# A routed-expert layer: one expert's overflow slots in straight code, the loop for all other overflow behind the last weight load

## The chip, the cores and the metric

The kernel runs on one core of a Trainium2 chip. The metric is the device time of one execution in microseconds (us), the median of several runs. The engines are PE (TensorE: matmuls; its weight loads are listed as PEld), DVE (VectorE), ACT (ScalarE), POOL (GpSimd) and SP (SyncE, which here only issues DMA transfers). Each engine works through its own queue of instructions in order, and engines wait for each other by semaphores.

## The reference

One decoder layer of 256 tokens and width 1024: a first sub-layer of token mixers, a cross-attention, and then the routed experts, which this change is about. Each token picks 4 of 32 experts:

```python
logits = (xf @ w_router) + b_router
top_val, top_idx = lax.top_k(logits, TOP_K)          # 4 of 32
gates = softmax(top_val)
# for each expert e, for the tokens that picked it:
h = x[tok] @ w1[e] + b1[e]                           # 1024 -> 2048
h_gate = min(h[:, :1024], 7); h_up = clip(h[:, 1024:], -7, 7)
act = h_gate * sigmoid(1.702 * h_gate) * (h_up + 1)
acc[tok] += (act @ w2[e] + b2[e]) * gate             # 1024 -> 1024
x = layer_norm(alpha * x + acc)
```

All is float32. The weights of one expert are 8 MB (w1) and 4 MB (w2).

## The kernel before

The experts are worked through in 16 pairs, in straight code. In its main pass each expert serves up to 64 tokens (`CAP`), its slots 1 to 64. A one-hot matrix `oh` (L1281) gathers the pair's tokens into `xg` (L1080), `expert_in` multiplies them with w1 (`pgt` and `pup`, L1103, with the bias first, L1097), `expert_swiglu` and `expert_turn` make the activation `at` on DVE, ACT and PE (L1119 to L1131), `expert_out` multiplies with w2 (`py`, L1144), and the pair's result goes into the accumulator `acc` by a matmul with the gates and an addition (`pc`, L1162 and L1163). In the last pair the accumulator is taken into the matmuls' own sums instead (`final`, `pc_last`, L1153 and L1158), and the last layer norm follows.

The weights come in pieces of 2 MB, six for an expert (four of w1, two of w2), into ten slots that are used in rotation (`RINGS`). SP issues all of these loads in order (L1023), each when the slot's former piece has been used. Behind the last piece stand two loads for the layer norm (`ln3`).

An expert may be picked by more than 64 tokens. Positions 2 to 31 are fixed, but which expert stands at position `PX` = 17 is decided at run time: the fullest one is swapped there (`swap`), so its overflow can be done while its weights are in the slots. Before, this was done in branches. At position 17, `overflow_in` (L1228) and `overflow_out` (L1271) run if its count exceeds 64: slots 65 to 96 by `extra_in` and `extra_out` (32 slots wide, tiles named with an `x` behind: `xsx`, `xtx`, `pgtx`, `pupx`, `pyx`, `pc0x`, `pc1x`), and, in an inner branch (L1229), five more blocks of 32 if it exceeds 96. After that pair `overflow_others` (L1240 to L1268) asks whether the highest count of the other experts exceeds 64 (L1241). Only then does a loop over the 32 experts run, which loads an expert's weights once more from POOL's queue and does its overflow in blocks. All five engines read the count (`tab_i`) and branch at L1241; an engine that doesn't enter jumps over its part of the loop's body, and adds to its semaphores what it left out.

Within straight code a scheduler decides each engine's order: it may issue a piece of work early where its inputs are ready. Across a branch it moves nothing.

Of the kernel before, what the change touches and what calls it, by code (L numbers as in the profile page):

```python
# [27 lines left out]
E = 32  # L28
# [19 lines left out]
def layer_kernel(ctx, tc, a, out, dbg=None):  # L48
# [955 lines left out]
    order = pool(ctx, "order")  # L1004

    Rp = order.tile([P, 2 * NT, E], F32, name="Rp")
    tab_i = order.tile([1, 2 * E + 2], I32, name="tab_i")
    cnt_i, idx_i = tab_i[:, 0:E + 2], tab_i[:, E + 2:]


    RINGS = [(ring2, "ring2")] * 3 + [(ring, "ring"), (ring3, "r0"), (ring3, "r1"), (ring, "ring"), (ring, "ring"),
# [28 lines left out]

    def w2_views(e):
        return [([P, 4, D], of(w2v, e)[c]) for c in range(2)]

    BRANCH = (mybir.EngineType.PE, mybir.EngineType.DVE, mybir.EngineType.Activation)

    class Main:

# [41 lines left out]
    def expert_in(v, sel, xg, chunks, nm, after=None):  # L1089


        n, W = v.n, v.W
        ps2 = v.gate("pgt" + nm), v.gate("pup" + nm)
        sel = sel.to_broadcast([3 * E, n])
        for i, ps in enumerate(ps2):
            for j in range(v.J):
                nc.tensor.matmul(ps[j * n:(j + 1) * n, :W], sel, b1[:, i * D + j * W:i * D + (j + 1) * W],  # L1097
                                 start=True, stop=False)
        for c, w in enumerate(chunks):
            for i, ps in enumerate(ps2):  # L1100
                for kk in range(2):
                    for j in range(v.J):
                        nc.tensor.matmul(ps[j * n:(j + 1) * n, :W], xg[:, 2 * c + kk, :],  # L1103
                                         w[:, kk, i * D + j * W:i * D + (j + 1) * W],
                                         start=False, stop=c == 3 and kk == 1)
            if after and c == 0:
                after()
        return ps2
# [17 lines left out]
    def expert_turn(v, hu, at, nm):  # L1126
        W = v.W
        pt = v.bank("pt" + nm)
        for u in range(W // P):
            nc.tensor.transpose(pt[:, u * P:(u + 1) * P], hu[:, u * P:(u + 1) * P], ident)  # L1130
        nc.scalar.activation(at, pt[:, :W], AF.Copy, scale=0.5)  # L1131
# [18 lines left out]
    def final(t, half, alloc):  # L1150

        finals[t, half] = ps = alloc(f"pc{t}{half}_last")
        nc.tensor.matmul(ps, ident, acc[:, t, half * 512:half * 512 + 512], start=True, stop=False)  # L1153

    def add_out(v, ct, y, rows, t, cols, nm):
        if finals:
# [48 lines left out]
    def extra_out(at, ct, w2, nm):  # L1205
        extra_add(expert_out(extra, at, w2, False, nm), ct, nm)
# [13 lines left out]
    def columns(e):  # L1220

        es = slice(e, e + 1)
        return Rp[:, 0:NT, es], Rp[:, NT:2 * NT, es], sel3p[:, es]

    def overflow_in(e, cnt, w1, w2):

        state = extra_tiles(f"x{e}")
        with tc.If(cnt > CAP):  # L1228
            with tc.If(cnt > CAP + 32):  # L1229
                for base in range(CAP + 32, T, 32):  # L1230
                    nm = f"x{e}_{base}"
                    extra_in(*columns(e), w1, base, *state, nm)
                    extra_out(*state, w2, nm)
            extra_in(*columns(e), w1, CAP, *state, f"x{e}")
        return state

    def overflow_others():

        pool = [mybir.EngineType.Pool]
        most = nc.values_load(cnt_i[0:1, E + 1:E + 2])  # L1240
        with tc.If(most > CAP):  # L1241
            with tc.For_i(0, E) as i:
                here = bass.ds(i, 1)
                cnt = nc.values_load(cnt_i[0:1, here])
                with tc.If(cnt > CAP):
                    idx = nc.values_load(idx_i[0:1, here], engines=pool, min_val=0, max_val=E - 1)
                    own = md.tile([P, 2 * NT, 1], F32, tag="own", bufs=1, name="own")
                    sel = md.tile([3 * E, 1], BF16, tag="ownsel", bufs=1, name="ownsel")
                    nc.vector.tensor_copy(own, Rp[:, 0:2 * NT, here])
                    nc.vector.tensor_copy(sel, sel3p[:, here])  # L1250

                    def again(nm, shape, view):
                        w = ring3.tile(shape, F32, tag="r3", name="again" + nm)
                        nc.gpsimd.dma_start(w, view)
                        return w

                    def block(base):
                        nm = f"z{base}"
                        state = extra_tiles(nm)
                        extra_in(own[:, 0:NT], own[:, NT:], sel, (again(nm, s, w) for s, w in w1_views(idx)), base,  # L1260
                                 *state, nm)
                        py = expert_out(extra, state[0], (again(nm, s, w) for s, w in w2_views(idx)), False, nm)
                        extra_add(py, state[1], nm)

                    block(CAP)
                    with tc.If(cnt > CAP + 32):
                        for base in range(CAP + 32, T, 32):
                            block(base)  # L1268

    def overflow_out(e, cnt, state, w2):  # L1270
        with tc.If(cnt > CAP):  # L1271
            extra_out(*state, w2, f"x{e}")

    def prepare(pr):

# [55 lines left out]

    swap(few[0:1], few[0:1])
    nc.vector.tensor_copy(idx_i, few[0:1, 0])
    nc.vector.tensor_copy(cnt_i[0:1, E:E + 1], few[0:1, 1, PX:PX + 1])
    nc.vector.memset(few[0:1, 1, PX:PX + 1], 0.0)
    nc.vector.tensor_copy(cnt_i[0:1, 0:E], few[0:1, 1])
    nc.vector.tensor_reduce(kmax[0:1], few[0:1, 1], axis=AX.X, op=OP.max)
    nc.vector.tensor_copy(cnt_i[0:1, E + 1:E + 2], kmax[0:1])

# [22 lines left out]
    for pr in range(E // 2):  # L1364
        xg, og, rest = nxt
        Y = [md.tile([P, 512], F32, tag=f"Y{i}", bufs=1, name=f"Y{i}_{pr}") for i in range(2)]
        for i in range(2):
            e = 2 * pr + i
            w1 = []
            ex = e if e < NS else nc.values_load(idx_i[0:1, e:e + 1], engines=[mybir.EngineType.SP], min_val=0,  # L1370
                                                 max_val=E - 1)
            for c, (sh, view) in enumerate(w1_views(ex)):
                w1.append(echunk(sh, view, f"w1_{e}_{c}"))
                if e == 1 and c == 0:
                    acc_start(*acc_load())
            w2 = [echunk(sh, view, f"w2_{e}_{c}", 4 if e == E - 1 and c else 1)
                  for c, (sh, view) in enumerate(w2_views(ex))]
            nm = f"{e}"
            cnt = nc.values_load(cnt_i[0:1, E:E + 1], engines=BRANCH) if e == PX else None
            if e == E - 1:  # L1380
                for t, half in ((0, 0), (0, 1), (1, 0)):
                    final(t, half, bank)
            ps2 = expert_in(main, (sel3 if e < NS else sel3p)[:, e:e + 1], xg[:, :, i * CAP:(i + 1) * CAP], w1, nm, rest if e == 0 else None)
            hu = expert_swiglu(main, ps2, nm)
            if e == E - 1:
                final(1, 1, gbank)
            at = main.tile("at" + nm)
            state = overflow_in(e, cnt, w1, w2) if e == PX else None

            with tc.issue_after(nc.cur_bb.bb.instructions[-1]) if e == PX else ExitStack():  # L1390
                expert_turn(main, hu, at, nm)
            if i == 0:
                cts = [md.tile([P, T], F32, tag=f"ct{j}", bufs=1, name=f"ct{j}_{pr}") for j in range(2)]
                for j in range(2):
                    gate_rows(main, og[:, :, j:j + 2].rearrange("p t a s -> p t (a s)"), cts[j], f"{pr}_{j}")
            py = expert_out(main, at, w2, i == 1, nm)
            for j in range(2):
                rows = slice(j * CAP, (j + 1) * CAP)
                nc.scalar.activation(Y[j ^ i][rows, :], py[rows, :], AF.Copy)  # L1399
            if i == 1:  # L1400
                if pr + 1 < E // 2:
                    nxt = prepare(pr + 1)
            if e == PX:
                overflow_out(e, cnt, state, w2)
        for t in range(NT):
            for half in range(2):
                add_out(main, cts[half], Y[half], slice(0, P), t, slice(half * 512, half * 512 + 512), f"{half}_{pr}")

        if pr == PX // 2:
            overflow_others()  # L1410

    ln3 = slot([P, 2, D], "ln3")
    nc.sync.dma_start(ln3[:, 0], a["ln3_g"].to_broadcast([P, D]))
    nc.sync.dma_start(ln3[:, 1], a["ln3_b"].to_broadcast([P, D]))
    st = md.tile([P, NT, 2, 6], F32, tag="ln_st", bufs=1, name="ln3st")
    for t in range(NT):
        for half in range(2):
# [76 lines left out]
```

## Time and profile before

| | |
|---|---|
| median of 3 runs | 1528.34 us (1526.82 to 1529.77) |
| profiled execution | 1527.18 us, span 1525.5 us, mean granted PE clock 0.977 |
| busy PE / PEld / DVE / ACT / POOL | 1396.3 / 778.6 / 577.1 / 427.3 / 8.8 us |
| moved by DMA | 480.21 MB, of it 475.72 MB in the queue that SP feeds |

All of the rows come from one profiled execution. Times in a timeline are us from the span's start; a timeline's row has start, length, engine, line, operation and tiles, and in brackets how long the engine stood idle before it and what released it. PE's matmuls overlap in a pipeline, so that starts tell more than lengths. L with a number is a line of the kernel.

### The profile page before, as it was taken

The numbers are of one execution on the slowest core, as the hardware profiler recorded it, in microseconds if no ns is written. First come the engines' busy times: TensorE is split into PE (matmuls) and PEld (weight loads), VectorE is DVE, ScalarE is ACT, GpSimd is POOL, SyncE is SP. The second block draws the span as 40 slices with busy tenths as digits, with TensorE's granted clock in tenths as the row PEclk, the third lists the DMA queues.
The fourth block names the chain that finished last, engine by engine and source line by source line (L and its number), as shares of the span: only waits on it lengthen the run. The fifth ranks groups of instructions, "written<-read, shape, count | busy, mean of one in ns | idle before, by whom it ended". The sixth has DMA issues, their size and how long they took to land. (4 is left out here: it accounts for less than half of the span.)

```text
span 1525.5 us, 21509 instructions
## 1 busy us (share of the span) xinstructions
PE 1396.3 (92%) x8749; PEld 778.6 (51%) x8750; DVE 577.1 (38%) x1434; ACT 427.3 (28%) x925; POOL 8.8 (1%) x25
## 2 busy tenths in 40 slices
PE   7999999999999999999999999978689889899895
PEld 6788978799988633333333333323223323323331
DVE  6587869667875532112112112111112112112113
ACT  6575757665574311101101101100001101101111
POOL 0000000000000000000000000000000000000000
PEclk9999999999999999999999999997899999999998
DMA  7243334266854899999999999990799999999995
GB/s 278 96 167 112 111 112 148 75 225 206 304 215 159 318 404 418 418 416 416 418 418 416 417 417 418 416 389 2 291 418 417 418 415 418 418 417 415 418 418 219
DMA packets 91290, 480.21 MB, mean 315 GB/s; under 512 B 4336, under 2 KB 6928, under 8 KB 56144
## 3 DMA queue, kind: packets, MB, share of 16 engines
q1 hardware_dynamic: 90368, 475.72, 78.0%
q0 software_dynamic: 816, 3.04, 0.7%
q8 instruction: 71, 1.16, 0.3%
q14 instruction: 35, 0.29, 0.1%
HBM read 477.69 MB, written 1.05 MB: 314 GB/s over the span
## 5 line engine op out<-in xcount | busy, mean ns | idle before, releaser
L1103 PE MATMUL pgt<-w,xg 128*64 128x512 f32 x1024 | 250.6, 602 | 36.3 <-DMA w<-in_w_exp_in_dram 36.3
L1144 PE MATMUL py<-w,at 128*64 128x512 f32 x1024 | 242.5, 623 | 14.7 <-ACT at L1131 14.7
L1103 PE MATMUL pup<-w,xg 128*64 128x512 f32 x1024 | 248.6, 598 | 0.0
L1119 DVE TENSOR_SCALAR hg<-pgt 128x512 f32<-128x512 f32 x32 | 22.1, 692 | 511.4 <-PE pgt L1103 511.4
L1103 PEld LDWEIGHTS pgt<-w,xg 128*64 128x64 f32 x1024 | 71.6, 137 | 191.6 <-issue 135.3
L1103 PEld LDWEIGHTS pup<-w,xg 128*64 128x64 f32 x1024 | 75.6, 139 | 149.2 <-issue 149.2
L1120 ACT ACTIVATE th<-hg 128x512 f32<-128x512 f32 x32 | 20.1, 629 | 469.7 <-DVE hg L1119 469.7
L1144 PEld LDWEIGHTS py<-w,at 128*64 128x64 f32 x1024 | 72.2, 142 | 154.2 <-issue 129.7
L1399 ACT ACTIVATE Y<-py 64x512 f32<-64x512 f32 x64 | 37.9, 592 | 180.4 <-PE py L1144 180.0
L1162 PE MATMUL pc<-Y,ct 128*128 128x512 f32 x120 | 55.4, 604 | 2.7 <-ACT Y L1399 2.7
L1131 ACT ACTIVATE at<-pt 128x512 f32<-128x512 f32 x32 | 19.1, 597 | 94.9 <-PE pt L1130 94.9
L1163 DVE TENSOR_TENSOR acc<-acc,pc 128x512 f32<-128x512 f32 x60 | 41.1, 685 | 8.2 <-PE pc L1162 6.5
L1097 PEld LDWEIGHTS <-sel3p 96*64 96x64 bf16 (+1 forms) x128 | 10.5, 109 | 52.3 <-issue 52.3
L1097 PE MATMUL pup<-b,sel3p 96*64 96x512 bf16 x60 | 12.2, 389 | 25.4 <-DVE hu L1122 25.4
L1162 PEld LDWEIGHTS pc<-Y,ct 128*128 128x128 f32 x120 | 21.6, 189 | 26.9 <-issue 14.8
L334 DVE SCALAR_TENSOR_TENSOR u<-ps_g,feat,u 128x255 f32<-128x255 f32 (+2 forms) x72 | 33.1, 474 | 0.3
L1130 PE MATMUL pt<-ident,hu 128*128 128x128 f32 x128 | 21.5, 290 | 10.2 <-DVE hu L1123 10.2
L1121 DVE SCALAR_TENSOR_TENSOR hg<-th,hg 128x512 f32<-128x512 f32 x32 | 22.1, 692 | 22.3 <-ACT th L1120 22.3
L230 PE MATMUL ps_g<-xT,wg_0h 128*128 128x256 f32 x96 | 28.1, 293 | 0.9 <-ACT wg_0h L219 0.9
L232 PE MATMUL ps_g<-xT,wg_0l 128*128 128x256 f32 x96 | 28.1, 293 | 0.3 <-DVE wg_0l L220 0.3
L231 PE MATMUL ps_g<-xT,wg_0h 128*128 128x256 f32 x96 | 28.0, 292 | 0.0
L230 PE MATMUL ps_g<-xT,wg_1h 128*128 128x256 f32 x96 | 27.8, 290 | 0.0
(944 smaller groups left out, 2535.5 us busy)
## 6 DMA issues: line engine op xcount, KB each, us to landing
w<-in_w_exp_in_dram SPq DMA_DIRECT2D x128, 2048.0 KB, 25.8
w<-in_w_exp_out_dram SPq DMA_DIRECT2D x63, 2048.0 KB, 31.0
w_g<-in_w_in_dram SPq DMA_DIRECT2D x7, 2048.0 KB, 7.7
w_d<-in_w_in_dram SPq DMA_DIRECT2D x4, 2048.0 KB, 7.8
w_gt<-in_w_in_dram SPq DMA_DIRECT2D x4, 2048.0 KB, 7.8
w_dv<-in_w_in_dram SPq DMA_DIRECT2D x2, 2048.0 KB, 12.2
w_diffo<-in_w_diff_o_dram SPq DMA_DIRECT2D x2, 2048.0 KB, 11.7
w_gdno<-in_w_gdn_o_dram SPq DMA_DIRECT2D x2, 2048.0 KB, 8.3
```

What stands on the lines that cost most here:

```text
L230: nc.tensor.matmul(ps, h[:, kk, :], src[0][:, k, :], start=k == 0, stop=False)
L231: nc.tensor.matmul(ps, h[:, kk, :], src[1][:, k, :], start=False, stop=False)
L232: nc.tensor.matmul(ps, l[:, kk, :], src[0][:, k, :], start=False, stop=k == KT - 1)
L334: m1 = nc.vector.scalar_tensor_tensor(y[:, sh:], ps[:, :T - sh], convw[:, blk, tau:tau + 1], y[:, sh:], op0=OP.mult, op1=OP.add)
L1097: nc.tensor.matmul(ps[j * n:(j + 1) * n, :W], sel, b1[:, i * D + j * W:i * D + (j + 1) * W], start=True, stop=False)
L1103: nc.tensor.matmul(ps[j * n:(j + 1) * n, :W], xg[:, 2 * c + kk, :], w[:, kk, i * D + j * W:i * D + (j + 1) * W], start=False, stop=c == 3 ...
L1119: nc.vector.tensor_scalar(hg, pgt, 7.0, None, op0=OP.min)
L1121: nc.vector.scalar_tensor_tensor(hg, th, 1.0, hg, op0=OP.add, op1=OP.mult)
L1144: nc.tensor.matmul(py[j * n:(j + 1) * n, :W], at[:, k % U, (k // U) * n:(k // U + 1) * n], w[:, kk, hf * W:(hf + 1) * W], start=k == 0, st ...
L1162: nc.tensor.matmul(pc, ct[rows, t * P:(t + 1) * P], y[rows], start=True, stop=True)
L1163: nc.vector.tensor_tensor(acc[:, t, cols], acc[:, t, cols], pc, op=OP.add)
L1399: nc.scalar.activation(Y[j ^ i][rows, :], py[rows, :], AF.Copy)
```

## The change

The extra block of position 17 (slots 65 to 96) stands in straight code and always runs; its count is no longer asked. What was in the inner branch, an own count over 96, is left to the loop for the others: the count of position 17 counts there if it exceeds 96 and is zero otherwise, and then the positions of its tokens up to 96 are set to zero so that they are not done twice. That loop, with its If, moves from behind pair 8 to the place in front of expert 31's matmuls, behind the issue of all weight loads and of the two norm loads. Its If is laid out with `preferred_fallthrough_block=False`: the path that doesn't enter the loop comes first, and leaves by a jump over the body. Expert 31's matmuls are queued behind the last of three `final` matmuls.

```diff
-    def overflow_in(e, cnt, w1, w2):
+    def overflow_in(e, w1):
         state = extra_tiles(f"x{e}")
-        with tc.If(cnt > CAP):
-            with tc.If(cnt > CAP + 32):
-                for base in range(CAP + 32, T, 32):
...
-            extra_in(*columns(e), w1, CAP, *state, f"x{e}")
+        extra_in(*columns(e), w1, CAP, *state, f"x{e}")
         return state
     def overflow_others():
-        most = nc.values_load(cnt_i[0:1, E + 1:E + 2])
-        with tc.If(most > CAP):
+        nc.vector.scalar_tensor_tensor(Rp[:, 0:NT, PX], Rp[:, 0:NT, PX], float(CAP + 32), Rp[:, 0:NT, PX],
+                                       op0=OP.is_gt, op1=OP.mult)
+        most = nc.values_load(cnt_i[0:1, E:E + 1])
+        with tc.If(most > CAP, preferred_fallthrough_block=False):
...
                     def again(nm, shape, view):
-                        w = ring3.tile(shape, F32, tag="r3", name="again" + nm)
+                        p, tag = RINGS[nslot[0] % len(RINGS)]
+                        w = p.tile(shape, F32, tag=tag, name="again" + nm)
-    def overflow_out(e, cnt, state, w2):
-        with tc.If(cnt > CAP):
-            extra_out(*state, w2, f"x{e}")
...
-    nc.vector.tensor_copy(cnt_i[0:1, E:E + 1], few[0:1, 1, PX:PX + 1])
-    nc.vector.memset(few[0:1, 1, PX:PX + 1], 0.0)
+    own = few[0:1, 1, PX:PX + 1]
+    nc.vector.scalar_tensor_tensor(own, own, float(CAP + 32), own, op0=OP.is_gt, op1=OP.mult)
...
-            cnt = nc.values_load(cnt_i[0:1, E:E + 1], engines=BRANCH) if e == PX else None
             if e == E - 1:
+                ln3 = slot([P, 2, D], "ln3")
+                nc.sync.dma_start(ln3[:, 0], a["ln3_g"].to_broadcast([P, D]))
+                nc.sync.dma_start(ln3[:, 1], a["ln3_b"].to_broadcast([P, D]))
+                overflow_others()
                 for t, half in ((0, 0), (0, 1), (1, 0)):
-                    final(t, half, bank)
-            ps2 = expert_in(main, ...)
+                    begun = final(t, half, bank)
+            with tc.issue_after(begun.ins) if e == E - 1 else ExitStack():
+                ps2 = expert_in(main, ...)
...
-            state = overflow_in(e, cnt, w1, w2) if e == PX else None
-            with tc.issue_after(nc.cur_bb.bb.instructions[-1]) if e == PX else ExitStack():
-                expert_turn(main, hu, at, nm)
+            state = overflow_in(e, w1) if e == PX else None
+            expert_turn(main, hu, at, nm)
...
-                overflow_out(e, cnt, state, w2)
+                extra_out(*state, w2, f"x{e}")
...
-        if pr == PX // 2:
-            overflow_others()
```

What SP's queue holds around the loop's If, before (TENSOR_LOAD reads the count; the L1242 to L1268 rows are the loop):

```order
L1370 TENSOR_LOAD tab_i
L1370 ISA x2
L1240 TENSOR_LOAD tab_i
L1241 COMPARE_AND_BRANCH
L1242 COMPARE_AND_BRANCH
...
L1241 UNCONDITIONAL_BRANCH
L1023 ISA
L1023 DMA w_18_0_11118<-in_w_exp_in_dram 128x2x2048
L1023 ISA
L1023 DMA w_18_1_11120<-in_w_exp_in_dram 128x2x2048
```

The first load of expert 18 stands behind the If. Now SP's queue, at its end:

```order
L1023 DMA w_31_1_10697<-in_w_exp_out_dram 128x1024
L1372 DMA ln_10702<-in_ln_g_dram 128x1024
L1373 DMA ln_10702<-in_ln_b_dram 128x1024
L1234 TENSOR_LOAD tab_i
L1235 COMPARE_AND_BRANCH
L1235 UNCONDITIONAL_BRANCH
L1236 COMPARE_AND_BRANCH
...
L1236 UNCONDITIONAL_BRANCH
L1416 DMA out_dram<-acc 128x512 x4
```

Only the four output stores are behind the If here. PE at expert 17, before, from its last piece of w1 on:

```order
L1103 MATMUL pup_8804<-w_17_3_8792,xg_8627 64x512 x4
...
L1379 TENSOR_LOAD tab_i
L1228 COMPARE_AND_BRANCH
L1229 COMPARE_AND_BRANCH
...
L1103 MATMUL pgtx_9735<-w_17_0_8786,xgx_9711 32x256 x8
L1103 MATMUL pupx_9736<-w_17_0_8786,xgx_9711 32x256 x8
...
L1271 COMPARE_AND_BRANCH
L1144 MATMUL pyx_9882<-w_17_0_8794,atx_8850 32x256 x16
...
L1144 MATMUL py_9827<-w_17_0_8794,at_8849 64x512 x8
```

All of the extra work stands between the branches, ahead of expert 17's own `py`. PE at the same place now:

```order
L1101 MATMUL pgt_8797<-w_17_0_8785,xg_8626 64x512 x4
L1101 MATMUL pup_8798<-w_17_0_8785,xg_8626 64x512 x4
L1101 MATMUL pgtx_8872<-w_17_0_8785,xgx_8848 32x256 x8
L1101 MATMUL pupx_8873<-w_17_0_8785,xgx_8848 32x256 x8
L1101 MATMUL pgt_8797<-w_17_1_8787,xg_8626 64x512 x4
...
L1142 MATMUL py_8964<-w_17_0_8793,at_8843 64x512 x7
...
L1142 MATMUL pyx_9018<-w_17_0_8793,atx_8844 32x256 x16
```

The extra matmuls stand directly behind the main ones of the same piece of weights, and `pyx` behind `py`. The gather of the extra tokens (`xsx`, `xtx`) and its bias moved further, to experts 1 and 2. PE in front of expert 31, before:

```order
L1097 MATMUL pup_12726<-b_5886,sel3p 64x512
L1130 MATMUL pt_12659<-ident,hu_12652 128x128 x4
...
L1144 MATMUL py_12675<-w_30_0_12608,at_12658 64x512 x8
L1153 MATMUL pc_last<-acc,ident 128x512 x3
L1144 MATMUL py_12675<-w_30_1_12610,at_12658 64x512 x8
L1103 MATMUL pgt_12725<-w_31_0_12704,xg_12545 64x512 x4
```

The three finals split expert 30's last product here, and expert 31's follows at once. The same place now (the bias products L1095 stood before in the gap while DVE made expert 30's activation):

```order
L1142 MATMUL py_10658<-w_30_1_10593,at_10641 64x512 x8
L1234 TENSOR_LOAD tab_i
L1235 COMPARE_AND_BRANCH
L1235 UNCONDITIONAL_BRANCH
...
L1151 MATMUL pc_last<-acc,ident 128x512 x3
L1095 LDWEIGHTS sel3p
...
L1101 MATMUL pgt_11865<-w_31_0_10687,xg_10528 64x512 x4
```

The If, the three finals and the bias products stand between expert 30's last product and expert 31's first.

More of the change, by code (lines that the diff above doesn't have):

```diff
@@ L1006, in layer_kernel @@
     Rp = order.tile([P, 2 * NT, E], F32, name="Rp")
-    tab_i = order.tile([1, 2 * E + 2], I32, name="tab_i")
-    cnt_i, idx_i = tab_i[:, 0:E + 2], tab_i[:, E + 2:]
+    tab_i = order.tile([1, 2 * E + 1], I32, name="tab_i")
+    cnt_i, idx_i = tab_i[:, 0:E + 1], tab_i[:, E + 1:]
     RINGS = [(ring2, "ring2")] * 3 + [(ring, "ring"), (ring3, "r0"), (ring3, "r1"), (ring, "ring"), (ring, "ring"),
@@ L1042, in w2_views @@
         return [([P, 4, D], of(w2v, e)[c]) for c in range(2)]
-    BRANCH = (mybir.EngineType.PE, mybir.EngineType.DVE, mybir.EngineType.Activation)
     class Main:
@@ L1152, in final @@
         finals[t, half] = ps = alloc(f"pc{t}{half}_last")
-        nc.tensor.matmul(ps, ident, acc[:, t, half * 512:half * 512 + 512], start=True, stop=False)
+        return nc.tensor.matmul(ps, ident, acc[:, t, half * 512:half * 512 + 512], start=True, stop=False)
     def add_out(v, ct, y, rows, t, cols, nm):
@@ L1223, in columns @@
         return Rp[:, 0:NT, es], Rp[:, NT:2 * NT, es], sel3p[:, es]
-    def overflow_in(e, cnt, w1, w2):
+    def overflow_in(e, w1):
         state = extra_tiles(f"x{e}")
-        with tc.If(cnt > CAP):
-            with tc.If(cnt > CAP + 32):
-                for base in range(CAP + 32, T, 32):
-                    nm = f"x{e}_{base}"
-                    extra_in(*columns(e), w1, base, *state, nm)
-                    extra_out(*state, w2, nm)
-            extra_in(*columns(e), w1, CAP, *state, f"x{e}")
+        extra_in(*columns(e), w1, CAP, *state, f"x{e}")
         return state
@@ L1333, in layer_kernel @@
     nc.vector.tensor_copy(idx_i, few[0:1, 0])
-    nc.vector.tensor_copy(cnt_i[0:1, E:E + 1], few[0:1, 1, PX:PX + 1])
-    nc.vector.memset(few[0:1, 1, PX:PX + 1], 0.0)
+    own = few[0:1, 1, PX:PX + 1]
+    nc.vector.scalar_tensor_tensor(own, own, float(CAP + 32), own, op0=OP.is_gt, op1=OP.mult)
     nc.vector.tensor_copy(cnt_i[0:1, 0:E], few[0:1, 1])
     nc.vector.tensor_reduce(kmax[0:1], few[0:1, 1], axis=AX.X, op=OP.max)
-    nc.vector.tensor_copy(cnt_i[0:1, E + 1:E + 2], kmax[0:1])
+    nc.vector.tensor_copy(cnt_i[0:1, E:E + 1], kmax[0:1])
     def acc_load():
@@ L1378, in layer_kernel @@
             nm = f"{e}"
-            cnt = nc.values_load(cnt_i[0:1, E:E + 1], engines=BRANCH) if e == PX else None
             if e == E - 1:
+                ln3 = slot([P, 2, D], "ln3")
+                nc.sync.dma_start(ln3[:, 0], a["ln3_g"].to_broadcast([P, D]))
+                nc.sync.dma_start(ln3[:, 1], a["ln3_b"].to_broadcast([P, D]))
+                overflow_others()
                 for t, half in ((0, 0), (0, 1), (1, 0)):
-                    final(t, half, bank)
-            ps2 = expert_in(main, (sel3 if e < NS else sel3p)[:, e:e + 1], xg[:, :, i * CAP:(i + 1) * CAP], w1, nm, rest if e == 0 else None)
+                    begun = final(t, half, bank)
+            with tc.issue_after(begun.ins) if e == E - 1 else ExitStack():
+                ps2 = expert_in(main, (sel3 if e < NS else sel3p)[:, e:e + 1], xg[:, :, i * CAP:(i + 1) * CAP], w1, nm,
+                                rest if e == 0 else None)
             hu = expert_swiglu(main, ps2, nm)
@@ L1407, in layer_kernel @@
                 add_out(main, cts[half], Y[half], slice(0, P), t, slice(half * 512, half * 512 + 512), f"{half}_{pr}")
-        if pr == PX // 2:
-            overflow_others()
-    ln3 = slot([P, 2, D], "ln3")
-    nc.sync.dma_start(ln3[:, 0], a["ln3_g"].to_broadcast([P, D]))
-    nc.sync.dma_start(ln3[:, 1], a["ln3_b"].to_broadcast([P, D]))
     st = md.tile([P, NT, 2, 6], F32, tag="ln_st", bufs=1, name="ln3st")
```

## The prediction

> **What bounds the kernel now.** I read part 2 of the page first, then the windows, the DMA queue's own waits, the branch instructions and the timeline. Part 2 (slices of 38 us) has the routed experts from slice 14 on:
>
> ```profile
> PE   7999999999999999999999999978689889899895
> ...
> DMA  7243334266854899999999999990799999999995
> GB/s 278 96 167 112 111 112 148 75 225 206 304 215 159 318 404 418 418 416 416 418 418 416 417 417 418 416 389 2 291 418 417 418 415 418 418 417 415 418 418 219
> ```
>
> The DMA engines run flat at 417 GB/s, except in one slice with 2 GB/s. The windows (stretch, length, busy us and instructions of PE, PEld, DVE, ACT and POOL, granted clock, DMA share, GB/s) show the hole's edges:
>
> ```profile
> 580.00:640.00 60.00, 56.53 (x268) 22.57 (x266) 14.21 (x31) 8.28 (x16) 0.00 (x0) 1.00 1.02 417
> 880.00:940.00 60.00, 56.52 (x266) 21.58 (x261) 12.48 (x26) 7.28 (x13) 0.00 (x0) 0.97 1.02 417
> 1000.00:1028.50 28.50, 21.25 (x98) 6.53 (x94) 2.78 (x5) 1.81 (x3) 0.00 (x0) 1.00 0.97 396
> 1028.50:1079.40 50.90, 39.92 (x314) 19.57 (x314) 11.39 (x28) 5.18 (x11) 0.00 (x0) 0.80 0.03 6
> 1079.40:1110.00 30.60, 20.75 (x88) 7.34 (x90) 4.06 (x10) 1.23 (x2) 0.00 (x0) 0.83 1.01 411
> 1110.00:1480.00 370.00, 330.07 (x1528) 124.75 (x1526) 67.47 (x138) 39.90 (x72) 0.00 (x0) 0.98 1.02 417
> ```
>
> Bytes not moved in the hole: (417 - 6) x 50.9 / 417 = 50.2 us of transfer; with its ramps (21 x 28.5 and 6 x 30.6 over 417) 52.0. Who stopped the queue is told by its own waits and by the branch rows (ns min/median/max, then start; PEldq is PE's sequencer):
>
> ```profile
> SPq L1023 <- PEq L1241: 60.9, 1, 60.9
> ```
>
> ```profile
> L1241 DVEq EVENT_SEMAPHORE  x2: 21/21/21, 1076.3 to 1076.4; - x2
> L1241 PEldq EVENT_SEMAPHORE  x2: 51/51/51, 1077.7 to 1077.9; - x2
> ...
> L1241 SPq COMPARE_BRANCH  x1: 53/53/53, 1015.9 to 1015.9; - x1
> ...
> L1241 PEldq COMPARE_BRANCH  x1: 3775/3775/3775, 1073.9 to 1073.9; - x1
> L1241 DVEq COMPARE_BRANCH  x1: 63/63/63, 1075.7 to 1075.7; - x1
> ```
>
> ```profile
> L1229 PEldq COMPARE_BRANCH  x1: 4215/4215/4215, 1026.1 to 1026.1; - x1
> ```
>
> ```profile
> L1228 PEldq COMPARE_BRANCH  x2: 86/136/185, 1026.0 to 1046.2; - x2
> ```
>
> SP reaches the loop's If at 1015.9, with every load of expert 17 issued, and its next load waits 60.9 us until PE has left that If at 1077.7. So the loads from expert 18 on wait for expert 17's whole overflow work.
>
> **Is PE or DMA the slower one?** PE's starts one pair of experts apart (twice), its first wait for a load, and two landings one pair apart (from the chain):
>
> ```profile
> 667.92 1.89 PE L1103 MATMUL pgt<-w,xg 128*64 128x512 f32 x8
> ...
> 724.00 1.89 PE L1103 MATMUL pgt<-w,xg 128*64 128x512 f32 x8
> ```
>
> ```profile
> 868.20 1.94 PE L1103 MATMUL pgt<-w,xg 128*64 128x512 f32 x8
> ```
>
> ```profile
> 925.98 1.94 PE L1103 MATMUL pgt<-w,xg 128*64 128x512 f32 x8
> ```
>
> ```profile
> 1010.71 1.94 PE L1103 MATMUL pgt<-w,xg 128*64 128x512 f32 x8 [1.04 <-DMA w<-in_w_exp_in_dram]
> ```
>
> ```profile
> 1163.48 28.59 DMA w<-in_w_exp_in_dram
> ...
> 1224.31 27.96 DMA w<-in_w_exp_in_dram
> ```
>
> A pair takes PE 56.1 us at full clock, 57.8 where 0.97 was granted; DMA takes (1224.31 + 27.96) - (1163.48 + 28.59) = 60.2. PE therefore gains 2.4 to 4.1 us a pair. It first waits for a load at 1010.71. Seven pairs earlier, at 580, it must have been 7 x 2.4 to 7 x 4.1 = 17 to 29 us behind, and the DMA ran at 417 GB/s there too. So PE may be that far behind without starving the queue.
>
> The overflow work of expert 17 on PE:
>
> ```profile
> 1030.95 1.93 PE L1189 MATMUL xsx<-x,ohx 128*32 128x256 f32 x16 [5.14 <-DVE ohx L1180]
> ...
> 1035.39 1.93 PE L1103 MATMUL pgtx<-w,xgx 128*32 128x256 f32 x16
> ...
> 1040.91 1.04 PE L1103 MATMUL pgtx<-w,xgx 128*32 128x256 f32 x16
> 1041.78 1.04 PE L1103 MATMUL pupx<-w,xgx 128*32 128x256 f32 x16
> ...
> 1047.04 3.66 PE L1144 MATMUL pyx<-w,atx 128*32 128x256 f32 x64 [0.29 <-ACT atx L1131]
> 1051.25 0.70 PE L1162 MATMUL pc0x<-yx,ctx 32*128 32x256 f32 x4 [0.55 <-ACT yx L1211]
> ...
> 1057.00 0.90 PE L1130 MATMUL pt<-ident,hu 128*128 128x128 f32 x3
> ```
>
> **Term 1: the hole closes, -50.2 us.** SP's queue now runs past expert 17 without an If. The bounds are 50.2 and 52.0; I take 50.2, as ramps also stand at the stream's ends.
>
> **Term 2: slots 65 to 96 in straight code, 0.** Its matmuls by group: weights of the first projection 8 x 0.87 = 7.0 (start to start 1040.91 to 1041.78), second 3.7, gather, transposes and bias 2 to 4.4 (1030.95 to 1035.39 was at half clock and with waits), additions at most 1057.00 - 1051.25 = 5.75, of which I take 4, since they now stand between the pair's own. The sum is 16.7 to 20.9; I take 17, and as the upper end the 26 from 1030.95 to 1057.00. About 3 of it is issued among experts 1 and 2, the rest in 17. The cover: PE then lies 17 us behind (26 at most), within the 17 to 29 that starved nothing; six pairs follow up to expert 30, worth 6 x 2.4 to 6 x 4.1 = 14 to 25, and PE's normal place in an even expert is some microseconds behind anyway. If the cover were gone, the rest would be added to the end: 0 expected, 9 to 12 in the worst corner. The shorter DVE table code (one operation for two) and the zeroing of a column on DVE sit beside PE: 0.
>
> **Term 3: the If in front of expert 31, +6.7 us.** On SP only the four output stores are queued behind it; the last loads and the two of the norm are ahead. POOL has nothing left. DVE and ACT next serve expert 31's gate. PE is the one that matters: behind its branch stand three final additions, four bias products and all of expert 31.
>
> ```profile
> 1470.13 0.39 PE L1097 MATMUL pgt<-b,sel3p 96*64 96x512 bf16 x2
> ...
> 1477.02 2.84 PE L1153 MATMUL pc_last<-acc,ident 128*128 128x512 f32 x6
> 1479.79 3.65 PE L1144 MATMUL py<-w,at 128*64 128x512 f32 x16
> 1483.27 1.89 PE L1103 MATMUL pgt<-w,xg 128*64 128x512 f32 x8
> ...
> 1486.70 1.89 PE L1103 MATMUL pgt<-w,xg 128*64 128x512 f32 x8
> ...
> 1494.69 1.94 PE L1103 MATMUL pgt<-w,xg 128*64 128x512 f32 x8 [0.95 <-DMA w<-in_w_exp_in_dram]
> ```
>
> In the time base of before (all of it 50.2 earlier now): expert 30's last product ends at 1480.6, since the finals no longer split it (2.8). PE falls through the comparison (0.1 to 0.2, as at L1228, where it did not jump), waits until its own matmuls are done (0.3), and jumps over the loop's body. The two jumps over such bodies cost PE 3.8 and 4.2 at the comparison that was taken; I take 4.2, since DMA is loaded here as it partly was at L1229. PE resumes at 1485.1, after 4.5 us of idleness. Then finals 2.8, bias 0.8 and three chunks of 3.43 (1483.27 to 1486.70 is one). After idleness PE starts slow:
>
> ```profile
> 1085.94 3.68 PE L1103 MATMUL pgt<-w,xg 128*64 128x512 f32 x8 [10.66 <-DMA w<-in_w_exp_in_dram]
> 1089.41 2.56 PE L1103 MATMUL pup<-w,xg 128*64 128x512 f32 x8
> 1091.81 1.88 PE L1103 MATMUL pgt<-w,xg 128*64 128x512 f32 x8
> ```
>
> Here 5.87 us went into what takes 3.43: +2.4, which I take again. The last chunk of expert 31's first projection then starts at 1485.1 + 2.8 + 0.8 + 10.3 + 2.4 = 1501.4 instead of 1494.69: 6.7 late. By then all weights have landed, and the rest follows as now.
>
> **Sum.** 1525.5 - 50.2 + 6.7 = 1482.0 of span; the profiled run took 1527.18, 1.7 more than its span, so 1483.7; the median 1528.34 lies 1.16 above it: **1484.8 us**.
>
> **Rivals.**
> - *The jump is nearly free* (0.10). DVE's jump took 0.06 and its next instruction came 0.6 later, and the jump that PE makes here has no condition; such a one over a long body has no row. PE would resume at 1481.4, stay warm, and reach the last chunk 0.6 late: 1478.7. [...]
> - *The fetch of code queues behind weights* (0.12). PE's jump was 0.44 dearer with 396 GB/s around it than in the hole. With the queue full it could wait for one more load, 60.2 / 12 = 5.0: 1489.8. [...]
> - *PE does not catch up* (0.06): overflow work of 26 with slow pairs leaves up to 9: 1494.
> - *The hole stays in part* (0.04): expert 17 holds six of the ten weight slots through its overflow work; if that takes 26, the four others cover 4 x 5.0 = 20, and DMA stops for 6: 1491.
> - *Slower* (0.02): the loop at the end is entered. It decides as soon as one count exceeds its limit. One block reads six 2 MB loads again, 30 us, and 32 passes with a jump of 3.8 cost 120: above 1620. Against it: no instruction of the loop ran before.
>
> My forecast, 1481 to 1487, has 0.66. A comparison of this kernel tells 0.2% (3 us) from no change. Faster 0.97, same 0.01, slower 0.02. The range 1478 to 1491 takes in the first two rivals.
>
> **What would show it.** No slice without DMA; SP's long wait gone; pgtx between the chunks of expert 17; PE without waits for loads for some pairs after it, and waiting again near expert 29; a PE gap of 4 to 5 us before the first pc_last, then matmuls at half speed for 3 to 4. I am wrong if that gap is below 1 or above 8, or if DMA pauses after expert 17.

## The result and the profile after

The changed kernel took 1485.51 us (median of 4 runs, 1485.08 to 1491.23), the kernel before 1527.62 beside it: a ratio of 0.9731, 95% interval 0.9705 to 0.9757. The forecast was 1484.8. The profiled execution has a span of 1484.2 us and a granted clock of 0.984.

Part 2 of the page of the changed kernel (slices of 37 us). From slice 16 to slice 39 the DMA row has no slice below full, at 414 GB/s or more: the slice with 2 GB/s is gone.

```profile
PE   7999999999999999999999999999999999989876
...
DMA  7343333354866689999999999999999999999992
GB/s 273 112 141 145 114 116 114 115 175 171 293 229 227 244 354 418 415 417 418 418 417 416 418 417 418 415 418 417 418 415 416 419 417 418 416 418 417 418 414 113
```

The waits of the DMA queue that issues the loads (who was waited for: total us, times, longest us). The wait of 60.9 us for PE's sequencer at the If no longer exists; the three largest of those left, for slots that PE's matmuls give back, are these, and no single one is above 18.8 us. (The view also puts one wait of 9.0 us down to the If in its new place; DMA is full there.)

```profile
SPq L1023 <- PE pup L1101: 265.9, 73, 17.6
SPq L1023 <- PE py L1142: 161.2, 28, 8.9
SPq L1023 <- PE pc L1160: 63.1, 12, 18.8
```

Expert 17 on PE (timeline: start, length, group of matmuls). The overflow groups pgtx and pupx now stand between the chunks of the main pass, and expert 18 starts at 1056.85, not at 1085.94.

```profile
1010.81 1.89 PE L1101 MATMUL pgt<-w,xg 128*64 128x512 f32 x8
1012.53 1.89 PE L1101 MATMUL pup<-w,xg 128*64 128x512 f32 x8
1014.35 1.07 PE L1101 MATMUL pgtx<-w,xgx 128*32 128x256 f32 x16
1015.23 1.05 PE L1101 MATMUL pupx<-w,xgx 128*32 128x256 f32 x16
...
1046.51 3.66 PE L1142 MATMUL pyx<-w,atx 128*32 128x256 f32 x64
...
1056.85 1.94 PE L1101 MATMUL pgt<-w,xg 128*64 128x512 f32 x8
```

Expert 18's first piece was issued at 1009.05 and took 28.9 us to land (views of the queue and of that one issue), so it lay there from about 1037.95 on, and PE, which starts on it at 1056.85, was 18.9 us behind. PE first waits for a load again in expert 25:

```profile
1009.05 9.40 SPq L1023 DMA_DIRECT2D w<-in_w_exp_in_dram  x1
```

```profile
w<-in_w_exp_in_dram SPq DMA_DIRECT2D x1, 2048.0 KB, 28.9
```

```profile
1255.23 1.94 PE L1101 MATMUL pgt<-w,xg 128*64 128x512 f32 x8 [0.84 <-DMA w<-in_w_exp_in_dram]
```

The end. First the branch rows of the If in front of expert 31 (ns min/median/max, first and last start), then PE's timeline through it. PE has two branch instructions there: the comparison (91 ns) at 1427.8, and, after a wait for its own matmuls (they end at 1431.6, the semaphore rows stand at 1431.7), the jump over the loop's body at 1432.1, which takes 6232 ns. The same two cost ACT 44 ns at most and DVE 55.

```profile
L1235 DVEq COMPARE_BRANCH  x2: 51/53/55, 1424.9 to 1425.3; - x2
...
L1235 PEldq COMPARE_BRANCH  x2: 91/3162/6232, 1427.8 to 1432.1; - x2
L1235 PEldq EVENT_SEMAPHORE  x2: 51/51/51, 1431.7 to 1431.9; - x2
L1235 ACTq COMPARE_BRANCH  x2: 38/41/44, 1432.2 to 1433.0; - x2
```

```profile
1424.52 7.09 PE L1142 MATMUL py<-w,at 128*64 128x512 f32 x32 [0.25 <-ACT at L1129]
1438.45 4.22 PE L1151 MATMUL pc_last<-acc,ident 128*128 128x512 f32 x6 [6.84 <-issue]
1442.61 0.41 PE L1095 MATMUL pgt<-b,sel3p 96*64 96x512 bf16 x2
...
1453.36 1.88 PE L1101 MATMUL pgt<-w,xg 128*64 128x512 f32 x8
```

PE does nothing for 6.84 us, then runs the final additions in 4.22 (2.84 before), and the last chunk of expert 31's first projection starts at 1453.36 instead of 1494.69: 41.3 us earlier, which is the whole gain of the span (1525.5 - 1484.2 = 41.3).

How much of that is the hole, and how much was given back? Expert 30 starts, in both kernels, in PE's steady place behind the loads:

```profile
1456.34 1.94 PE L1103 MATMUL pgt<-w,xg 128*64 128x512 f32 x8
```

```profile
1407.44 1.94 PE L1101 MATMUL pgt<-w,xg 128*64 128x512 f32 x8
```

That is 48.9 us earlier (before, then after). So the closed hole brought 48.9, and the If in front of expert 31 gave 48.9 - 41.3 = 7.6 back.

### The profile page after: what moved, and what is told of

It reads as the page before. It is cut to its first block, busy times and chain, and to the rows that moved or that the text cites. A ratio compares the mean times of both kernels' runs of the same rounds, so it can differ in the third digit from the quotient of the medians.

```text
span 1484.2 us, 21484 instructions
## 1 busy us (share of the span) xinstructions
PE 1386.1 (93%) x8749; PEld 776.0 (52%) x8750; DVE 577.1 (39%) x1434; ACT 427.3 (29%) x925; POOL 8.8 (1%) x25
## 3 DMA queue, kind: packets, MB, share of 16 engines
q8 instruction: 71, 1.16, 0.3%
## 5 line engine op out<-in xcount | busy, mean ns | idle before, releaser
L1101 PE MATMUL pgt<-w,xg 128*64 128x512 f32 x1024 | 247.3, 597 | 9.0 <-DMA w<-in_w_exp_in_dram 9.0
L1101 PE MATMUL pup<-w,xg 128*64 128x512 f32 x1024 | 246.2, 595 | 0.0
L1101 PEld LDWEIGHTS pgt<-w,xg 128*64 128x64 f32 x1024 | 71.7, 137 | 157.9 <-issue 139.8
L1101 PEld LDWEIGHTS pup<-w,xg 128*64 128x64 f32 x1024 | 74.4, 138 | 147.1 <-issue 147.1
L1095 PEld LDWEIGHTS <-sel3p 96*64 96x64 bf16 (+1 forms) x128 | 9.8, 108 | 49.1 <-issue 49.0
L1095 PE MATMUL pup<-b,sel3p 96*64 96x512 bf16 x60 | 12.1, 389 | 22.8 <-DVE hu L1120 22.8
```

## The experiments

All times are medians of 5 runs (4 in one case), compared with runs of the kernel before on the same chip. Three theories are at stake. *Slot*: the loads behind pair 8 stopped because the first of them takes the slot that the loop names. *Queue*: an If on the way of the issuing queue, or expert 17's branches, stops them. *Fetch*: PE's jump is dear because the code at its target has to come by DMA first.

**1. The kernel before, one statement changed: the loop's weights take the slot that was filled last, which comes up again only at the tenth load.**

```diff
-  w = ring3.tile(shape, F32, tag="r3", name="again" + nm)
+  p, tag = RINGS[(nslot[0] - 1) % len(RINGS)]
+  w = p.tile(shape, F32, tag=tag, name="again" + nm)
```

> The kernel before with one thing changed: the loop's weights tile lies in the slot that was filled last, not in the one that the next load takes. Theory slot (the loads behind pair 8 waited for PE's end of the loop's If only because the first of them takes the slot that the loop names): SP's wait of 60.9 us goes, the hole shrinks to a few us (PE leaves expert 17 about 42 us behind the weights, more than the 29 that starved nothing), and PE, 21 us later at expert 18 than in the changed kernel, makes up all but some 4 of it: about 1490 us (1484 to 1497). Theory queue (an If that SP has to walk through, or the branches of expert 17, stop SP's loads by themselves): as before, 1527 us.

Measured: 1487.77 us, ratio 0.9746 (0.9732 to 0.9759). The branches, the loop and its place are as before, and SP walks through the same If, at 1020.0. Three loads of expert 18 are now issued ahead of it, and the six after them don't wait for PE's end of the If either. The wait for it now comes at the tenth load, the fourth piece of expert 19, and is 11.8 us long; the row of GB/s falls to 349 in one slice.

```profile
SPq L1023 <- PEq L1241: 11.8, 1, 11.8
```

```profile
GB/s 283 102 164 121 115 115 114 115 175 188 304 227 227 246 362 417 416 418 417 418 416 417 417 418 416 416 418 417 349 406 416 417 418 418 415 417 418 418 416 138
```

So the slot made the hole. This edit alone brings 39.6 us, where the whole change brought 42.1, and the intervals of the two ratios overlap.

**2. The changed kernel, with the loop behind pair 8 again, its weights in the slot filled last.**

```diff
-  p, tag = RINGS[nslot[0] % len(RINGS)]
+  p, tag = RINGS[(nslot[0] - 1) % len(RINGS)]
...
-                overflow_others()                    # in front of expert 31
...
+        if pr == PX // 2:
+            overflow_others()
```

> The changed kernel, but the loop stands behind pair 8 again and its weights tile lies in the slot that was filled last. Theory slot: no hole, PE pays its jump (4 to 6 us) at expert 18, where it is then 23 to 25 us behind the weights, which starves nothing, and makes it up by expert 30, so nothing of the jump is left at the end: 1478 to 1480 us. If PE does not make it up: 1482 to 1486. Theory queue: a hole of about 30 us, 1508 us.

Measured: 1480.5 us, ratio 0.9693 (0.968 to 0.9706). The jump is as long as at the end (6010 ns), but PE has the experts up to 31 to make it up (in the profiled run the last chunk starts at 1448.65, 4.7 us earlier than in the changed kernel), and SP's next load that needs the loop's slot waits 4.9 us, with others in the queue:

```profile
L1235 PEldq COMPARE_BRANCH  x2: 95/3052/6010, 1057.4 to 1059.9; - x2
```

```profile
SPq L1023 <- PEq L1235: 4.9, 1, 4.9
```

**3. The same place, but the slot that the next load takes.** 

```diff
-                overflow_others()
...
+        if pr == PX // 2:
+            overflow_others()
```

> The changed kernel, but the loop stands behind pair 8 again, and its weights tile lies in the slot that the next load takes, as in the kernel before. Theory slot: expert 18's first piece is issued when PE has left the loop's If, at about 1062 instead of 1009, and lands about 8 us later, 32 us later than in the changed kernel; SP shows a wait of 45 to 55 us there; the end pays no jump: about 1510 us (1503 to 1515). If only the length of the old overflow work in branches made the hole: 1478 to 1486.

Measured: 1506.94 us (4 runs), ratio 0.9866 (0.985 to 0.9881). The hole is back, without any branch in expert 17, and shorter (40.3 us, where 45 to 55 were expected), because PE reaches the If sooner. PE waits there for the load that waited for PE:

```profile
SPq L1023 <- PEq L1235: 40.3, 1, 40.3
```

```profile
1064.56 3.68 PE L1101 MATMUL pgt<-w,xg 128*64 128x512 f32 x8 [9.25 <-DMA w<-in_w_exp_in_dram]
```

Kernels 2 and 3 differ in the slot alone: 26.4 us. Theory queue falls.

**4. The changed kernel without the loop and its If.**

```diff
-                overflow_others()
```

> The changed kernel without the loop and its If (these inputs never enter it). Theory jump: the last chunk of expert 31's first projection starts when it lands and not 6.0 us later, and if the fetch of the jump's target also held up that landing (6.57 us behind the one before it, others 4.98), 1.6 more: 1478 to 1480 us. If the end waits for something else, 1485 us.

Measured: 1479.42 us, ratio 0.9684 (0.9671 to 0.9698): the If at the end costs 6.1 us by the medians of the two kernels (1485.51), 7.0 against kernel 11, the same kernel on this chip (1486.44), and 7.3 by the profiled spans (1484.2 and 1476.9). The last chunk starts at 1446.09, 1.99 us behind the group before it, where the others follow one another at 1.72 (I take the 0.27 between for the wait for its piece), and PE's matmuls before it have their usual length:

```profile
1444.10 1.92 PE L1101 MATMUL pup<-w,xg 128*64 128x512 f32 x8
1446.09 1.94 PE L1101 MATMUL pgt<-w,xg 128*64 128x512 f32 x8
```

Kernel 2, with the loop, is within 1.1 us of it: there the loop costs nothing that these runs can tell (the intervals overlap).

**5. One block in the loop instead of all.**

```diff
                     block(CAP)
-                    with tc.If(cnt > CAP + 32):
-                        for base in range(CAP + 32, T, 32):
-                            block(base)
```

> The changed kernel; the loop in front of expert 31 holds one block of 32 slots (65 to 96) and not all of them, so the code that PE jumps over is a fraction of what it was (the others are left out; these inputs never enter the loop). Theory fetch (the jump waits until code that was not fetched ahead has come by DMA, behind weights): one block is still longer than what PE has fetched ahead, so the jump takes about 6 us again, 1485 us. Theory length (the time grows with the code that is jumped): 1 to 2 us, 1480 us.

Measured: 1488.19 us, ratio 0.9746 (0.9733 to 0.976), no gain, and the jump as long as over the full body:

```profile
L1235 PEldq COMPARE_BRANCH  x2: 95/3054/6014, 1429.6 to 1433.8; - x2
```

**6. No block in the loop.**

```diff
-                    block(CAP)
-                    with tc.If(cnt > CAP + 32):
-                        for base in range(CAP + 32, T, 32):
-                            block(base)
```

> The changed kernel; the loop in front of expert 31 keeps its conditions and its run over the experts, but its blocks are left out (these inputs never enter it), so PE jumps over a few instructions. Both theories of the jump: the target has been fetched, the jump takes under 0.5 us, PE's gap before the first final addition falls from 6.84 to 1 to 2 us, 1479 to 1481 us. If a jump on PE costs its 6 us for any distance: 1485 us.

Measured: 1479.68 us, ratio 0.9689 (0.9676 to 0.9703). The longer of PE's two branches takes 193 ns:

```profile
L1235 PEldq COMPARE_BRANCH  x2: 90/142/193, 1457.0 to 1457.3; - x2
```

In this kernel the finals and expert 31's first projection stand ahead of the If on PE, so the time isn't a clean price of the distance. The branch rows are a better one, though DMA was probably idle when PE came there at 1457.0: the last slice of this run's page, from 1440.9 on, has 159 GB/s, that is 5.9 MB, which 417 GB/s move in 14 us (an estimate). A far jump with 17 GB/s around it still took 3.3 us (below). Together with kernel 5: one block costs as much as six, and none costs next to nothing. So the time doesn't grow with the body beyond one block, and a limit lies somewhere between no block and one (the same block at position 17 of the kernel before has 238 matmuls and as many weight loads).

**7. The straight-line overflow work twice.**

```diff
+        extra_in(*columns(e), w1, CAP + 32, *state, f"y{e}")
         extra_in(*columns(e), w1, CAP, *state, f"x{e}")
...
                 extra_out(*state, w2, f"x{e}")
+                expert_out(extra, state[0], w2, False, f"y{e}")
```

> The changed kernel with the straight-line overflow work of the fullest expert done twice (the second time for slots 97 to 128, which are empty, with the first and the second projection, without the additions): 12 to 14 us more of PE. By the steps of the prediction PE is then about 32 us behind the weights at expert 18, a little over the 29 that starved nothing, makes up 19 to 20 by expert 30 and comes there some 4 us late: 1489 us (1487 to 1493). If the cover is larger than I think: 1485. If PE's work there is not hidden at all: 1498.

Measured: 1489.69 us, ratio 0.9753 (0.9738 to 0.9767). Expert 18 starts 10.3 us later than in the changed kernel (12 to 14 were expected):

```profile
1067.17 1.07 PE L1101 MATMUL pgt<-w,xg 128*64 128x512 f32 x2
```

From 1225 to 1445 no matmul waits for a load, so PE no longer comes back to its steady place. The middle of the forecast for this kernel was met, but its interval touches that of the changed kernel (0.9705 to 0.9757); only the trace tells the two apart.

**8. The changed kernel without that work.**

```diff
-            state = overflow_in(e, w1) if e == PX else None
...
-            if e == PX:
-                extra_out(*state, w2, f"x{e}")
```

> The changed kernel without the straight-line overflow work of the fullest expert (its slots 65 to 96 are left out of the output). By the prediction this work is hidden behind the weights: 1485 us, with PE waiting for loads from expert 18 or 19 on. If it is not hidden: 1471 us.

Measured: 1487.26 us, ratio 0.9729 (0.9716 to 0.9743), the same as with it. PE waits for loads from expert 19 on, and gains nothing by it:

```profile
1068.02 1.94 PE L1101 MATMUL pgt<-w,xg 128*64 128x512 f32 x8 [0.78 <-DMA w<-in_w_exp_in_dram]
```

**9. The move alone: the loop in front of expert 31, the branches of expert 17 as before.**

```diff
-            state = overflow_in(e, w1) if e == PX else None
+            state = overflow_in(e, cnt, w1, w2) if e == PX else None
...
-                extra_out(*state, w2, f"x{e}")
+                overflow_out(e, cnt, state, w2)
```

> The other half of the change alone: the loop stands in front of expert 31, and expert 17 keeps its branches as in the kernel before. No hole but a few us (PE some 40 us behind at expert 18, as in the kernel with the other slot, where 11.3 us of it were left at expert 31), and then the jump of 6 us with its slow restart at the end: 1494 us (1491 to 1499), that is some 9 us above the changed kernel. If the straight code is worth nothing at the end (all of its gain hidden): 1485.

Measured: 1496.33 us, ratio 0.9795 (0.9781 to 0.9808). PE starts expert 18 at 1075.52, as late as the branches of the kernel before let it, does not make that up by expert 31, and pays the jump on top. (This kernel's lines are shifted by some rows; L1151 and L1101 are the same statements.)

```profile
1075.52 1.94 PE L1101 MATMUL pgt<-w,xg 128*64 128x512 f32 x8
...
1447.75 5.46 PE L1151 MATMUL pc_last<-acc,ident 128*128 128x512 f32 x6 [6.54 <-issue]
```

**10. The changed kernel without its choice of layout.**

```diff
-        with tc.If(most > CAP, preferred_fallthrough_block=False):
+        with tc.If(most > CAP):
```

> The changed kernel without its choice of layout: the comparison itself jumps over the loop's body, and no second jump follows. By the theory that the fetch of the target sets the time, the jump takes about 6 us as well: 1485 us, no difference. If the choice of layout was worth something: 1487 or more; if it cost something: 1480 to 1483.

Measured: 1482.52 us, ratio 0.9708 (0.9694 to 0.9721); the changed kernel, run beside it, had 1486.44 and 0.9738 (0.9725 to 0.9752). I expected no difference, and there is one of 3.9 us. The jump is as long, but it starts earlier:

```profile
L1235 PEldq COMPARE_BRANCH  x1: 6077/6077/6077, 1426.4 to 1426.4; - x1
```

```profile
1423.20 7.09 PE L1142 MATMUL py<-w,at 128*64 128x512 f32 x32 [0.25 <-ACT at L1129]
1433.04 4.47 PE L1151 MATMUL pc_last<-acc,ident 128*128 128x512 f32 x6 [2.75 <-PEq L1235]
```

The sequencer takes the comparison at 1426.4, while PE still has 3.9 us of expert 30's products in its queue (until 1430.29). Their time covers the first part of the jump, and PE is idle for 2.75 us instead of 6.84. In the changed kernel a semaphore of the If stands between comparison and jump, and PE's sequencer passes it only when its matmuls are done (1431.7, in the rows above): the whole jump is then idle time.

**11 and 12. The changed kernel and kernel 2 once more, side by side.**

> The changed kernel once more, beside the next one: 1485 us, PE's jump 6 to 6.3 us.

> Straight code in expert 17, loop behind pair 8 with its weights in the slot filled last, once more beside the changed kernel: 1480.5 us, 4 to 6 us faster than the changed kernel, since the same jump is paid where PE has time to make it up.

Measured: 1486.44 us, ratio 0.9738 (0.9725 to 0.9752), and 1479.69 us, ratio 0.9687 (0.9674 to 0.97). The version with the loop left behind pair 8 beats the changed kernel by 6.8 us, more than the 4 to 6 expected, and the intervals are apart. Not tried: kernel 2 with the layout of kernel 10.

## Why the prediction was right, point by point

- *Term 1, the hole, -50.2.* Measured 48.9 at expert 30; why not the full 50.2 is open. The reading of the wait was right: SP's loads waited for PE at that If. What the prediction left open is by what they waited. It said that SP's queue "now runs past expert 17 without an If", as if the If had to go. Kernels 1 to 3 show that the If may stay; the slot that its loop names had to go. Moving the loop closes the hole too, but costs time of its own (kernels 11 and 12).
- *Term 2, overflow work in straight code, 0.* Right: leaving it out changes nothing (kernel 8). PE was 18.9 us behind at expert 18, where 17 was forecast, and caught up by expert 25, earlier than the forecast place near expert 29. Straight code against branches is another matter, which the sum never priced apart: with the loop behind pair 8 it is worth 1487.77 - 1480.5 = 7.3 us (kernels 1 and 2, one chip), and with the loop at the end 1496.33 - 1486.44 = 9.9 (kernels 9 and 11, one chip), since PE comes out of the branches some 19 us later (1075.52 against 1056.85) and can't make that up.
- *Term 3, the If in front of expert 31, +6.7.* Measured 7.6. The jump was the mis-sized part: 6.23, not 4.2. The gap was 6.84, not 4.5 (right by the bounds of 1 and 8 that were set). The slow restart was cheaper: the finals took 4.22 instead of 2.84 (granted clock 0.66 there), so +1.4 and not +2.4, and the chunks behind them ran at full speed (granted clock 1.00). The gap's +2.3 and the restart's -1.0 partly cancel. Expert 30's last product ended at 1424.52 + 7.09 = 1431.6, 1.2 later than the 1430.4 that the hole of 50.2 gave; that is Term 1's miss, seen here.
- *The sum.* Span 1482.0 forecast, 1484.2 measured: 1.3 from Term 1, 0.9 from Term 3. That the median came within 0.7 us of the forecast is partly luck: the forecast put the median 1.16 above the profiled run, as before, and this time it lay 0.3 below it (1485.51 and 1485.83). The four runs spread over 6 us.
- *Rivals.* The free jump fell (6232 ns), and so did the hole that stays and the PE that doesn't catch up. The fetch behind weights was half right: the direction, and 2.0 of its 5.0 us. PE's far jumps, with what DMA moved meanwhile, make that plain. Two in the kernel of experiment 1:

```profile
L1241 PEldq COMPARE_BRANCH  x1: 3317/3317/3317, 1073.2 to 1073.2; - x1
...
L1229 PEldq COMPARE_BRANCH  x1: 6055/6055/6055, 1023.6 to 1023.6; - x1
```

Windows of the same kernel over these two (busy us of the engines, granted clock, DMA share, GB/s):

```profile
1023.60:1029.60 6.00, 0.00 (x0) 0.00 (x0) 0.00 (x0) 0.00 (x0) 0.00 (x0) 0.63 1.03 413
1073.20:1076.50 3.30, 2.33 (x6) 0.45 (x4) 1.77 (x3) 0.00 (x0) 0.00 (x0) 1.00 0.05 17
```

With DMA at 413 GB/s the jump takes 6.06, with 17 GB/s 3.32. In the kernel before, 3.78 fell in the hole (6 GB/s), and the 4.22 that I took for "loaded" ran at the edge of the hole (the window from 1026.1 to 1030.3 has 143 GB/s). That is the error: the row was not of a full queue. The same jump at L1229 took 6.06 in experiment 1, where the queue was full. Full queues add 2.2 to 2.9 us (6.0 to 6.23 against 3.78 and 3.32). The traces also show something of where the time goes: within each of three far jumps, two in the kernel before and one in the changed kernel, a packet of 0.02 MB moves on the queue that the DMA view lists as `q8 instruction`. With DMA idle it moves 0.9 us after the jump's start (at 1074.8, 6 GB/s), at the edge of the hole 1.8 us (at 1027.9, 143 GB/s), with DMA full 3.5 us (at 1435.6 in the changed kernel, 416 GB/s), and in all three the jump is over 2.4 to 2.9 us later. I read the packet as the code at the jump's target, which stands in wait while the weights move; no run shows what it carries. In a whole execution that queue moves 71 packets in the changed kernel and in kernel 5, 69 in kernel 6, whose jump is short, and 69 in kernel 4, which has no loop. On the length, kernels 5 and 6 agree with theory fetch: 6014 ns over one block, 193 over none.

## What to carry to other kernels

When loads stop at a conditional block, look first at which buffer the block names: here a tile in the slot that the very next load needed made the queue wait until PE had left the block, though no engine entered it, and another slot of the ring freed the queue with one statement. A jump over a body of code cost PE 6 us here under a full DMA queue, so place it where PE has time to make it up, not in front of the last work, and let PE reach it with matmuls still queued. Take the price of an operation from a row that ran under the same load as the place you move it to.

## What the hardware showed that I had not expected

- PE's jump over a body of code took 6.0 to 6.25 us wherever DMA was at 400 GB/s or more (408 to 419 in the windows of kernels 1, 2 and 10 and of the changed kernel), for one block or six, and 3.3 to 4.4 in or at the edge of a hole of the DMA queue (6 to 278 GB/s). A packet of the queue `q8 instruction` moved 3.5 us after the jump's start at 416 GB/s and 0.9 in an idle hole. DVE and ACT paid under 0.08 us for the same Ifs.
- A jump of PE's sequencer runs beside matmuls that are already queued: 6.08 us cost 2.75 of idle time (kernel 10). A semaphore ahead of the jump that waits for PE's own matmuls takes this cover away: 6.23 cost 6.84 (the changed kernel).
